# Four units' query scores in one group, a 16-bit pair look-up, both attentions' queries by token

## The chip, the cores and the metric

The program runs on one core of one Trainium2 chip. A core has a matrix engine (PE, TensorE; its weight loads are PEld), a vector engine (DVE), a scalar engine (ACT), GpSimd (POOL) and SyncE (SP), which here only issues DMAs. Each engine takes its instructions strictly in the order of its own queue and waits on semaphores. The metric is the device time of one execution in microseconds; lower is better.

## The reference

Two transformer layers follow each other on 256 tokens of width 1024, in fp32. The change touches the first.

```python
h = concat([meta_tokens(16), x(256), zeros])                      # 272 tokens count
proj = rms_norm(h, attn_norm) @ w_in                              # c_q, c_kv, k_rope, dq, dk, dv
y_mla  = softmax(rope(norm(q)) @ rope(norm(k)).T * s) @ v         # 8 heads of 96, q from c_q (256 wide)
y_diff = (softmax(q1 k1 + bias) - lam * softmax(q2 k2 + bias)) @ v   # 4 heads, 2 x 64 each, q = norm(dq)
h = h + concat([y_mla, y_diff]) @ w_out
# PEER, on xn = rms_norm(h):
q = (xn @ w_query).reshape(.., 8, 2, 128)                         # 8 heads, two sides
s = einsum(q, sub_keys)                                           # 128 keys a side
s1, i1 = top_k(s[side 0], 16);  s2, i2 = top_k(s[side 1], 16)
best, flat = top_k(s1[:, None] + s2[None, :], 16)                 # of 256 sums
e1 = take(i1, flat // 16);  e2 = take(i2, flat % 16)              # the look-up
act = gelu(xn . u[e1 * 128 + e2]);  h = h + (softmax(best) * act) . v[...]
```

The queries of all heads (q of the MLA, dq of the differential attention) are wanted for 256 tokens, the keys for 272. `take` picks, for each of 128 slots of a token and each side, one of 16 indices.

## The kernel before

The weights stream through in 399 units of 512 KB. `unit` (called for each) issues the DMA into `raw` (4 buffers), ACT or DVE rounds it to fp32r as `wh`, and DVE or POOL makes the rest `wl = raw - wh` (3 buffers each). A product of fp32 accuracy is three fp32r products (`mm3`: hi*hi, hi*lo, lo*hi). A unit of the kind `_stat` is stationary and yields features on partitions (moving operand: 256 or 272 tokens); one of the kind `_mov` is the moving operand (512 columns) and yields tokens on partitions.

Stages in order of time: the input products and both attentions (0 to 165 us); `wq`, the PEER queries in 16 units (169 to 227 us); 90 of the 128 `u` units, with the routing (top 16 and look-up) and then the gates beside them on DVE; the other `u` and all `v` units; then the second layer.

`Flow` records every operation (so all of them have line 683) and `schedule` writes each engine's queue before the run: it walks a model time, takes for each engine the ready operation of the lowest priority (place in the program, some biases), with costs from `_cost`. `ORDER` is the program order of the attention's generators (`dq`, `q`, `m`, `V` are the diff queries, MLA queries, MLA heads, dv units). `Side` lays pieces of a generator between the `u` units: each `yield` gives a rough cost, and `side.step(2.1)` grants so much per unit.

What the change touches:

- `pair_norm("dq")`: 4 stationary units; for each the square on ACT, two fp32 products with 2 columns for the sums by head, then spreading of the norms by transposes (PE) and 4 multiplications (DVE).
- `queries`: per MLA head 6 products with `uq` stationary, a DVE multiplication with the rope table, a square on ACT, two one-column fp32 products for the sums.
- `values` and `mla_head`: the values of the first 16 keys stand on partitions 0 to 15 of `mv[:, 0]`. For each head the weights of these keys are transposed (2 transposes into the g bank), copied by DVE, and multiplied with `mv[:, 0]` (2 fp32 products of 64 columns), beside 3 transposes and 3 products for the other keys; then a reciprocal and a scaling.
- `wq`: after each unit ACT copies the result to `t`, and 2 fp32 products with the sub-keys write the scores (`s<-s,t`); ACT takes the scores out after every fourth unit.
- `routing`: look-up per half of the tokens and side: `is_equal` (128x2048 fp32), a product with the indices (128x2048 fp32), a sum over 16.
- `tok_norm` (3 calls with `rows`): `squares` leaves two halves, and `total` adds them in PE with 4 one-column products.

Of the kernel before, what the change touches and what calls it, by code (L numbers as in the profile page):

```python
# [125 lines left out]
def _units(i):  # L126
# [3 lines left out]
    kr = w[:, 512:544]  # L130
    kr = np.concatenate([kr, kr[:, _SWAP]] * 2, 1)
    r = uq[:, :, 64:]
    r = np.concatenate([r, r[:, :, _SWAP]], 2)
    even, odd = np.concatenate([uq[:, :, :64], r], 2), np.concatenate([r, uq[:, :, :64]], 2)
    uq = np.concatenate([(odd if h % 2 else even)[:, h] for h in range(8)], 1)
# [8 lines left out]
    return {  # L144
        "dk": _stat(w[:, 1056:1568]), "dq": _stat(w[:, 544:1056]), "dv": np.concatenate([_mov(w[:, 1568:1824]), _mov(w[:, 1824:2080])], 0),
        "ckv": _stat(w[:, 256:512]), "kr": _stat(kr), "cq": _stat(w[:, 0:256]),
        "ukn": _stat(c(ukv[:, :, :64]).reshape(256, 512)), "uv": _mov(c(ukv[:, :, 64:]).reshape(256, 512)),
        "uq": _stat(uq), "woa": _stat(wo[:512]), "wob": _stat(wo[512:]),
        "xk": _stat(kv[:, :256]), "xv": _mov(kv[:, 256:]),
# [18 lines left out]
def _vec_list(i):  # L168
# [9 lines left out]
    two = lambda v: np.concatenate([v, v])[:, None]  # L178
    rope = lambda v: np.concatenate([v[64:], v[64:][_SWAP]] * 2)[:, None]
    rb = np.zeros((P, 4), np.float32)  # L180
# [44 lines left out]
def _consts():  # L225
# [19 lines left out]
    cos, sin = np.cos(ang).T, np.sin(ang).T  # L245
    e["cs"] = np.concatenate([cos, cos, -sin, sin] * 2, 0).astype(f)
    d = S - 1 - np.arange(NR)
# [131 lines left out]
class Flow:  # L379
# [129 lines left out]
    def schedule(self):  # L509
# [53 lines left out]
        while done < len(ops):  # L563
            progress = False
            for e in self.real:
# [128 lines left out]
def _build(tc, nc, ctx, A, O):  # L694
# [378 lines left out]
    def values():  # L1073
        wh, wl = mov(unit("uv"), 512)
        for c in range(3):
            o = bank("d")
            for k in range(2):
                mm3(o, ckh[:, k, VC[c]], ckl[:, k, VC[c]], wh[:, k], wl[:, k], k == 0, k == 1)
            if c == 0:
                G.memset(mv[:, 0], 0.0)  # L1080
            n = P if c else NM
            SC.activation(mv[:n, c], o[:n], AF.Copy)
            yield


    mr = sm(32)

    def queries():
        acc = bank("g")
        for h in range(8):  # L1090
            if h % 4 == 0:
                wh, wl = unit("uq")
            o = bank("d")[:, :T]
            for k in range(2):
                mm3(o, wh[:, 2 * (h % 4) + k], wl[:, 2 * (h % 4) + k], cqh[:, k], cql[:, k], k == 0, k == 1)
            V.tensor_mul(mq[:, h], o, tq[h % 2])
            q = square(o, T)
            for c, sl in enumerate(TT):
                PE.matmul(acc[:, 8 * c + h:8 * c + h + 1], q[:, sl], c_("indb" if h % 2 else "inda"),
                          start=h == 0 and c == 0, stop=h == 7 and c == 1, skip_group_check=True)  # L1100
            yield
        inv_sqrt(mr[:, 0:16], acc[:, :16], 1.0, E96)
        V.tensor_scalar(mr[:, 16:32], mr[:, 0:16], -1.0, None, op0=OP.mult)
        yield

    lam = sm(8)
# [37 lines left out]
    def mla_head(hd):  # L1144
        w = tmp[:, 1056 * (hd % 4):1056 * (hd % 4) + 1056]
        s, st = bank("s"), fl.tile([P, 16], F32, "hs")
        es = []
        for q in range(2):
            n = NB[q]
            sq = s[:, 144 * q:144 * q + n]  # L1150
            PE.matmul(sq, mq[:, hd, TT[q]], mk[:, hd, :n], start=True, stop=True)
            e = w[:, 144 * q:144 * q + n]
            soft(e, sq, mask[:, S - n:S], mr[:, 16 + 8 * q + hd:17 + 8 * q + hd], st[:, q:q + 1], st[:, 2 + q:3 + q])
            es.append(e)
        V.reciprocal(st[:, 4:6], st[:, 2:4])
        b = bank("g")
        weigh(b, 256, 64, es[0], es[1], mv, slice(64 * hd, 64 * hd + 64), w)
        z = st[:, 4:6].rearrange("p (c f) -> p c f", (P, 2, 1), f=1).to_broadcast([P, 2, 64])
        V.tensor_tensor(om[:, :, 64 * hd:64 * hd + 64], by_head(b[:, 256:384], 2, 64), z, op=OP.mult)

# [71 lines left out]
    def mla_heads():  # L1232
        for hd in range(8):
            mla_head(hd)
            if hd % 2:
                mla_out(hd // 2)
            yield
# [17 lines left out]
    def half_dense(*args):  # L1255
        for _ in half_units(*args):
# [3 lines left out]
    parts = {"dk": pair_norm("dk", dk, gd[:, 0:1], ALL, S, VC, KT, em, "s"),  # L1260
             "dq": pair_norm("dq", dq, 0.125, XS, T, TT, QT, em[:, 1:3], "p"), "k": keys(), "v": values(), "q": queries(),
             "K": rotated(), "C": latents(), "b": distances(), "L": lambdas(), "m": mla_heads(), "V": dv_units(),
# [39 lines left out]
    ab_i = small[:, 1536:2048].bitcast(U32)  # L1302
    i1f, abf = small[:, 2048:2560], small[:, 2560:3072]
    e12, wgt = small[:, 3072:3584], small[:, 3584:3840]
    one_i32 = c_("iota")

    def slots(j, n=1):
# [9 lines left out]

    ps_s = None
# [25 lines left out]
    def routing():  # L1344
        for c in range(2):
            for g in range(16):
                o = 256 * c + 16 * g
                top16(s_[c][:, g], s1[:, o:o + 16], i1[:, o:o + 16])
                yield 1.0
            V.tensor_copy(i1f[:, 256 * c:256 * c + 256], i1[:, 256 * c:256 * c + 256])  # L1350
            sv = s1[:, 256 * c:256 * c + 256].rearrange("p (h s k) -> p h s k", (P, 8, 2, 16), h=8, s=2)
# [12 lines left out]
            V.tensor_copy(abf[:, 256 * c:256 * c + 256], ab_i[:, 256 * c:256 * c + 256])  # L1364
            iv = i1f[:, 256 * c:256 * c + 256].rearrange("p (h s k) -> p h s k", (P, 8, 2, 16), h=8, s=2)
            for side in range(2):
                x = abf[:, 256 * c + 128 * side:256 * c + 128 * side + 128]
                hot = cand[c].flat.rearrange("p (s j) -> p s j", (P, 128, 16), s=128)
                V.tensor_tensor(hot, one_i32[:, 0:16].rearrange("p (o j) -> p o j", (P, 1, 16), o=1).to_broadcast([P, 128, 16]),
                                x.rearrange("p (s o) -> p s o", (P, 128, 1), o=1).to_broadcast([P, 128, 16]), op=OP.is_equal)  # L1370
                yield 2.3
                cv = cand[c].flat.rearrange("p (h a b) -> p h a b", (P, 8, 16, 16), h=8, a=16)
                V.tensor_tensor(cv, cv, iv[:, :, side, :].rearrange("p h (o k) -> p h o k", (P, 8, 1, 16), o=1)
                                .to_broadcast([P, 8, 16, 16]), op=OP.mult)
                yield 2.3
                V.reduce_sum(out=e12[:, 256 * c + 128 * side:256 * c + 128 * side + 128], in_=hot, axis=AX.X)
                yield 2.3
# [546 lines left out]
```

## Time and profile before

| what | value |
|---|---|
| median of 3 runs | 1346.52 us (1344.83 to 1346.79) |
| the profiled execution: its own time, its span | 1346.25 us, 1344.1 us |
| PE, DVE, ACT, POOL busy | 1324.5, 978.6, 722.1, 65.9 us |
| chain that ended last | PE 87%, DVE 7%, the rest 1% each or less |
| mean granted clock of PE | 0.997 of full speed |

PE's busy time is the union of its instructions, each shown from its start to its modelled end. Since they are pipelined, neighbours overlap: the distance between starts is what an instruction costs PE, and the recorded 0.28 us of a product is more than that. A product of two fp32 operands (not fp32r) appears as two records; a transpose as one. Where a wait is under some tenths of a microsecond, it is seen only as a larger distance between starts, not as idle time.

### The profile page before, as it was taken

To read this page: it belongs to the slowest core of one execution; us is meant where nothing else is said; L and a number is where in the kernel's file an instruction comes from. 1 tells how busy PE (TensorE), PEld (TensorE's weight loads), DVE (VectorE), ACT (ScalarE), POOL (GpSimd) and SP (SyncE) were. 2 spreads that over 40 slices of the span, in tenths; PEclk is the share of its full clock that TensorE was granted. 3 is DMA by queue.
4 is the path that set the end of the run, shared out by engine and by line. 5 is a ranking of instruction groups with operands and counts; after the bars stand their busy time and mean duration, and the time that the engine had idled before them with its cause. 6 is when DMAs were issued, how large, how long until landed. Compare 5 with 4: busy or idle time off the path is not lost.

```text
span 1344.1 us, 23753 instructions
## 1 busy us (share of the span) xinstructions
PE 1324.5 (99%) x9270; PEld 1205.1 (90%) x9270; DVE 978.6 (73%) x1833; ACT 722.1 (54%) x1222; POOL 65.9 (5%) x31
## 2 busy tenths in 40 slices
PE   9999999999999999999999999999999999999997
PEld 8898899999999999889999888888889798999996
DVE  7555789998498877985655555575576678978886
ACT  6445545435466665454544444444555546755555
POOL 0000001445200000000000000000000000000000
PEclk9999999999999999999999999999999999999999
DMA  6342344555587779995655555575545244465553
GB/s 236 120 143 79 108 145 143 171 184 180 171 282 258 259 267 347 364 309 188 202 188 189 187 188 187 187 249 187 186 163 185 82 152 153 144 198 185 177 184 98
DMA packets 101048, 256.29 MB, mean 191 GB/s; under 512 B 7940, under 2 KB 42696, under 8 KB 100808
## 3 DMA queue, kind: packets, MB, share of 16 engines
q1 hardware_dynamic: 95216, 236.62, 54.2%
q10 hardware_dynamic: 5720, 18.17, 3.4%
q8 instruction: 72, 1.18, 0.4%
q14 instruction: 40, 0.33, 0.1%
HBM read 236.86 MB, written 17.83 MB: 189 GB/s over the span
## 4 chain that ended last, share of the span: by engine, by line
PE 87%; DVE 7%; DMA 1%; ACT 1%; issue 1%; ACTq 0%; DVEq 0%
PE d L683 30%; PE acc L683 26%; PE g L683 5%; PE ua L683 4%; PE ug L683 4%; PE facc L683 4%; DVE s L683 4%; PE s L683 3%; PE wq L683 3%; DVE wl L683 2%; PE p L683 2%; DMA raw<-st 1%; PE dq L683 1%; PE mq L683 1%; PE mk L683 1%
## 5 line engine op out<-in xcount | busy, mean ns | idle before, releaser
L683 DVE TENSOR_TENSOR wl<-raw,wh 128x1024 fp32r<-128x1024 f32 x385 | 474.0, 1233 | 188.8 <-ACT wh L683 187.3
L683 ACT ACTIVATE wh<-raw 128x1024 fp32r<-128x1024 f32 x399 | 420.9, 1056 | 350.6 <-PE d L683 193.2
L683 PE MATMUL d<-ah,wl 128*128 128x256 f32 x1088 | 308.7, 284 | 3.9 <-DVE wl L683 3.6
L683 PE MATMUL d<-ah,wh 128*128 128x256 f32 x1088 | 309.9, 285 | 0.4 <-DVE h L683 0.3
L683 PE MATMUL d<-al,wh 128*128 128x256 f32 x1088 | 307.8, 283 | 0.8 <-DVE al L683 0.8
L683 PEld LDWEIGHTS d<-ah,wl 128*128 128x128 f32 x1088 | 205.9, 189 | 6.3 <-DVE wl L683 5.1
L683 PEld LDWEIGHTS d<-ah,wh 128*128 128x128 f32 x1088 | 206.0, 190 | 2.3 <-DVE h L683 0.7
L683 PEld LDWEIGHTS d<-al,wh 128*128 128x128 f32 x1088 | 205.9, 189 | 2.1 <-DVE al L683 1.0
L683 PE MATMUL acc<-wh,ch 128*128 128x512 f32 x512 | 203.4, 397 | 0.0
L683 PE MATMUL acc<-wl,ch 128*128 128x512 f32 x512 | 203.4, 397 | 0.0
L683 PE MATMUL acc<-wh,cl 128*128 128x512 f32 x512 | 202.2, 395 | 0.0
L683 ACT ACTIVATE ch<-s 128x256 fp32r<-128x256 f32 x149 | 62.0, 417 | 170.0 <-PE acc L683 166.6
L683 DVE TENSOR_TENSOR cl<-s,ch 128x256 fp32r<-128x256 f32 x149 | 63.2, 425 | 76.0 <-ACT ch L683 75.8
L683 PEld LDWEIGHTS acc<-wh,cl 128*128 128x128 f32 x512 | 96.5, 188 | 23.4
L683 PEld LDWEIGHTS acc<-wh,ch 128*128 128x128 f32 x512 | 96.5, 189 | 22.8
L683 PEld LDWEIGHTS acc<-wl,ch 128*128 128x128 f32 x512 | 96.4, 188 | 21.5
L683 POOL TENSOR_TENSOR wl<-raw,wh 128x1024 fp32r<-128x1024 f32 x22 | 61.9, 2814 | 287.5 <-PE wq L683 222.1
L683 DVE TENSOR_TENSOR s<-s,s 128x256 f32<-128x256 f32 (+5 forms) x142 | 55.8, 446 | 0.5 <-ACT s L683 0.3
L683 DVE TENSOR_TENSOR s<-s 128x2048 f16<-128x2048 f16 (+4 forms) x47 | 53.3, 1136 | 0.8
L683 POOL TENSOR_TENSOR s<-s 128x512 f32<-128x512 f32 x2 | 2.5, 1284 | 983.3 <-ACT s L683 983.3
L683 ACT ACTIVATE s<-d 128x512 f32<-128x512 f32 (+1 forms) x71 | 41.4, 583 | 15.4 <-PE d L683 15.3
L683 PE MATMUL ua<-al,wh 128*128 128x256 f32 x168 | 47.6, 283 | 0.2 <-DVE al L683 0.2
(307 smaller groups left out, 2374.4 us busy)
## 6 DMA issues: line engine op xcount, KB each, us to landing
raw<-st SPq DMA_DIRECT2D x407, 512.0 KB, 3.6
gd<-u ACTq DMA_DIRECT2D x32, 512.0 KB, 5.2
s<-gd SPq DMA_DIRECT2D x16, 1024.0 KB, 8.8
h<-xt SPq DMA_DIRECT2D x2, 512.0 KB, 6.5
s<-sk SPq DMA_DIRECT2D x1, 1024.0 KB, 5.0
u<-mt SPq DMA_DIRECT2D x4, 256.0 KB, 4.9
o<-s SPq DMA_DIRECT2D x3, 256.0 KB, 2.9
s<-ear SPq DMA_DIRECT2D x1, 664.0 KB, 6.2
```

Of the source, the lines that this page charges most:

```text
L683: f(*[real(a) for a in o.args], **{k: real(a) for k, a in o.kw.items()})
```

## The change

1. `wq`: the scores of four units are computed after the fourth, 8 products in a row.
2. Look-up: indices and one-hot rows are fp16, two slots interleaved (`iot` holds each number twice), so that `is_equal` and the product work on 128x2048 fp16; the sum reads the pairs with a stride and writes fp32 as before. The side grants are 1.75 per unit in the routing and 2.4 in the gates (both 2.1 before).
3. `queries` and `diff_queries`: `uq` and `dq` are moving operands. The MLA queries come out by token (two units of 512 columns), DVE copies them, ACT squares, DVE sums by head, then 16 transposes bring each head back to features, and DVE multiplies with the rope table from PSUM. The diff queries accumulate in two p banks over four units, are normed by two DVE multiplications, transposed (8) and copied out by ACT.
4. `values`: the first 32 key columns stand four times side by side, so the values of the first keys land on the partitions 32i to 32i+15. `mla_head` lays down four heads' results in one g bank; after the fourth, the four heads' first-key weights are gathered (2 DVE copies), transposed (2), copied, and multiplied in 2 products of 256 columns; one reciprocal and one scaling serve four heads.
5. `tok_norm` with `rows`: DVE adds the two halves of the squares, PE has 2 one-column products instead of 4.
6. `ORDER` follows the new yields; the planner adds 130 ns to single-input DVE operations while POOL works.

```diff
-ORDER = "... dk dk k v b k v q k v q dk dk dq q q dq q q dq q dk dk dq q q dq dq m dq m m dq m V m m V ..."
+ORDER = "... dk dk k v b k v q k v q dk dk dq q dq q dq dk dk dq q q dq m dq m m dq m V m m V ..."
+                elif e == "v" and o.meth in SINGLE and shared["g"] > now:
+                    cost += 130.0
@@ tok_norm
         sq = squares(x, T, KD, 2, r[:, 2:3])
+        if rows:
+            V.tensor_add(sq[0], sq[0], sq[1])
+            sq = sq[:1]
@@ queries
-            o = bank("d")[:, :T]
-            for k in range(2):
-                mm3(o, wh[:, 2 * (h % 4) + k], wl[:, 2 * (h % 4) + k], cqh[:, k], cql[:, k], k == 0, k == 1)
+            for c in range(2):
+                o = bank("d")
+                for k in range(2):
+                    mm3(o, cqh[:, k, TT[c]], cql[:, k, TT[c]], wh[:, k], wl[:, k], k == 0, k == 1)
+                V.tensor_copy((om, oo)[u][:, c], o)
+                at = 8 * c + 4 * u
+                by_head_sums(o, acc[:, at:at + 4].rearrange("p (a b) -> p a b", (P, 2, 2), a=2), 4, 128, paired)
...
+            for c in range(2):
+                PE.transpose(o[:, TT[c]], (om, oo)[h // 4][:, c, P * (h % 4):P * (h % 4) + P], ident)
             V.tensor_mul(mq[:, h], o, tq[h % 2])
-            q = square(o, T)
-            for c, sl in enumerate(TT):
-                PE.matmul(acc[:, 8 * c + h:8 * c + h + 1], q[:, sl], c_("indb" if h % 2 else "inda"),
@@ mla_head, after the fourth head (i == 3)
+            for c in range(2):
+                PE.transpose(pm[:, TT[c]], ml[:, TT[c]], ident)
+            V.tensor_copy(pms, pm)
+            for c in range(2):
+                PE.matmul(b[:, T * c:T * c + T], pms[:, TT[c]], mv[:, 0, at:at + T], start=False, stop=c == 1, ...)
@@ wq
-        if g % 4 == 0:
-            ps_s = [bank("s") for _ in range(2)]
-        for c in range(2):
-            PE.matmul(ps_s[c][:, (g % 4) * P:(g % 4 + 1) * P], qt[:, TT[c]], skt[:, g], start=True, stop=True)
-        if g % 4 == 3:
+        qts.append(qt)
+        if g % 4 == 3:
+            ps_s = [bank("s") for _ in range(2)]
+            for c in range(2):
+                for i in range(4):
+                    PE.matmul(ps_s[c][:, i * P:i * P + P], qts[g - 3 + i][:, TT[c]], skt[:, g - 3 + i], start=True, stop=True)
@@ routing, look-up
-                V.tensor_tensor(hot, one_i32[:, 0:16]...to_broadcast([P, 128, 16]), x...to_broadcast([P, 128, 16]), op=OP.is_equal)
+                V.tensor_tensor(hot, iot[:, 0:16]...to_broadcast([P, 64, 16, 2]), x, op=OP.is_equal)
-        side.step(2.1)
+        side.step(2.4 if side.gates else 1.75)
```

Where the instructions move. First PE in the middle of `wq`: `wq` rows are products of a unit, `s<-...,t` the scores. Before:

```order
L683 MATMUL wq<-ah,wh 128x256
L683 MATMUL wq<-al,wh 128x256
L683 MATMUL s<-s_1440,t 128x128 x2
L683 MATMUL wq<-ah,wl 128x256
L683 MATMUL wq<-ah,wh 128x256
```

and now:

```order
L685 MATMUL wq<-al,wh 128x256
L685 MATMUL wq<-ah,wl 128x256
L685 MATMUL s<-s_1293,t 128x128 x8
L685 MATMUL wq<-ah,wh 128x256
L685 MATMUL wq<-al,wh 128x256
```

The scores of a unit stood two products into the next one, 16 times; the scores of four units now stand right behind the last product of the fourth, four times.

Second DVE at the first look-up, early in the `u` units (`s_1440` and `s_1293` hold the sums and then the one-hot rows, `s_1975` and `s_1846` the indices and results; a `wl` is the split of a weight unit that PE waits for). Before:

```order
L683 TENSOR_TENSOR wl<-raw,wh 128x1024
L683 TENSOR_TENSOR s_1440<-s_1440,s_1975 128x2048
L683 TENSOR_REDUCE s_1975<-s_1440 128x128
L683 TENSOR_TENSOR wl<-raw,wh 128x1024
L683 TENSOR_TENSOR s_1440<-cst,s_1975 128x2048
L683 TENSOR_TENSOR wl<-raw,wh 128x1024
L683 TENSOR_TENSOR s_1440<-s_1440,s_1975 128x2048
L683 TENSOR_REDUCE s_1975<-s_1440 128x128
L683 TENSOR_TENSOR wl<-raw,wh 128x1024
```

and now:

```order
L685 TENSOR_TENSOR wl<-raw,wh 128x1024
L685 TENSOR_TENSOR s_1293<-s_1293,s_1846 128x2048
L685 TENSOR_REDUCE s_1846<-s_1293 128x128
L685 TENSOR_TENSOR wl<-raw,wh 128x1024
L685 TENSOR_TENSOR s_1293<-iot,s_1846 128x2048
L685 TENSOR_TENSOR s_1293<-s_1293,s_1846 128x2048
L685 TENSOR_REDUCE s_1846<-s_1293 128x128
L685 TENSOR_TENSOR wl<-raw,wh 128x1024
```

The second side's three operations now stand between two splits, where a split stood between the first and the second of them; counted from the start of `wq` the first multiplication comes one DVE split later.

Third PE among the MLA heads (`p<-cst` and `g<-cst` are transposes, `g<-s_71,s_123` the products with the values, `d<-w..` the dv units). Before:

```order
L683 MATMUL g<-s_71,s_123 128x64 x5
L683 MATMUL p<-cst,s_123 128x128 x2
L683 MATMUL g<-cst,s_123 128x128
L683 MATMUL p<-cst,s_123 128x128 x3
L683 MATMUL d<-wh,s_104 128x256 x2
L683 MATMUL p<-cst,s_123 128x128 x2
L683 MATMUL g<-s_71,s_123 128x64 x5
```

and now, at the end of the first four heads:

```order
L685 MATMUL g<-s_71,s_123 128x256 x2
L685 MATMUL d<-wl,s_104 128x256
L685 MATMUL p<-cst,s_123 128x128
L685 MATMUL d<-wh,s_104 128x256
L685 MATMUL s<-s_71 128x272
L685 MATMUL p<-cst,s_123 128x128 x2
L685 MATMUL g<-cst,s_71 128x128 x4
```

Each head had five products of 64 columns; now it has three, and two of 256 columns serve four heads. The four transposes `g<-cst,s_71` of the heads' outputs stand one scaling (DVE) behind them.

## Rows read from the trace of the kernel before

**Rows 1.** The page: busy time, share of the span and records of each engine.
```profile
PE 1324.5 (99%) x9270; PEld 1205.1 (90%) x9270; DVE 978.6 (73%) x1833; ACT 722.1 (54%) x1222; POOL 65.9 (5%) x31
```

**Rows 2.** Stretches: length, busy PE, PEld, DVE, ACT, POOL (records), clock, DMA, GB/s.
```profile
87.00:125.00 38.00, 37.99 (x309) 36.37 (x309) 22.02 (x79) 20.19 (x57) 0.00 (x0) 1.00 0.34 109
155.00:160.00 5.00, 4.86 (x26) 4.65 (x26) 2.30 (x6) 1.17 (x3) 0.00 (x0) 0.66 0.36 105
169.00:226.00 57.00, 57.00 (x452) 53.93 (x452) 51.39 (x220) 28.14 (x48) 1.95 (x1) 1.00 0.46 149
226.00:277.00 51.00, 47.60 (x397) 46.99 (x396) 50.93 (x158) 25.59 (x32) 20.65 (x9) 1.00 0.49 155
360.00:510.00 150.00, 150.00 (x1513) 149.31 (x1512) 125.21 (x110) 90.77 (x191) 0.00 (x0) 1.00 0.75 258
775.00:800.00 25.00, 25.00 (x108) 20.12 (x107) 14.59 (x19) 12.32 (x18) 0.00 (x0) 1.00 0.57 188
```

**Rows 3.** PE by form: out<-in, shape xcount | busy us, mean ns | idle before.
```profile
L683 PE MATMUL s<-s,t 128*128 128x128 f32 x64 | 11.4, 301 | 0.4 <-ACT t L683 0.4
...
L683 PE MATMUL g<-s,s 128*128 128x64 f32 x80 | 9.7, 270 | 0.0
...
L683 PE MATMUL g<-cst,t 128*128 128x1 f32 x36 | 4.9, 240 | 0.0
```

**Rows 4.** PE among the MLA heads: start, us, engine, what xcount.
```profile
93.53 0.62 PE L683 MATMUL s<-s 128*128 128x272 f32 x2
93.99 0.27 PE L683 MATMUL p<-cst,s 128*128 128x128 f32 x1
94.10 1.23 PE L683 MATMUL g<-s,s 128*128 128x64 f32 x10
```

**Rows 5.** PE in `wq`, one unit's period.
```profile
192.26 0.71 PE L683 MATMUL s<-s,t 128*128 128x128 f32 x4
...
192.93 0.28 PE L683 MATMUL wq<-ah,wh 128*128 128x256 f32 x1
...
195.54 0.28 PE L683 MATMUL wq<-al,wh 128*128 128x256 f32 x1
195.82 0.38 PE L683 MATMUL s<-s,t 128*128 128x128 f32 x1
```

**Rows 6.** The chain of waits at the look-up: start, us, what.
```profile
214.86 2.02 DVE s L683 x9
...
267.33 1.90 DVE wl L683
...
273.68 3.02 DVE wl L683
```

**Rows 7.** PE in the `u` units at the look-up; idle before, and its releaser.
```profile
269.29 0.39 PE L683 MATMUL d<-ah,wl 128*128 128x256 f32 x1 [1.50 <-DVE wl L683]
...
276.74 0.39 PE L683 MATMUL d<-ah,wl 128*128 128x256 f32 x1 [1.49 <-DVE wl L683]
```

**Rows 8.** DVE by form: the look-up, the gates, the splits.
```profile
L683 DVE TENSOR_TENSOR wl<-raw,wh 128x1024 fp32r<-128x1024 f32 x385 | 474.0, 1233 | 188.8 <-ACT wh L683 187.3
...
L683 DVE TENSOR_TENSOR s<-iot,s 128x2048 f16<-128x2048 f16 x32 | 37.8, 1218 | 0.0
...
L683 DVE TENSOR_TENSOR s<-cst,s 128x2048 f32<-128x2048 f32 x4 | 11.1, 2785 | 0.0
...
L683 DVE TENSOR_REDUCE s<-s 128x128 f32<-128x2048 f32 x4 | 9.1, 2286 | 0.1
L683 DVE TENSOR_TENSOR s<-s 128x2048 f32<-128x2048 f32 x4 | 9.1, 2280 | 0.0
```

**Rows 9.** POOL's split and DVE's first `is_equal`, side by side.
```profile
260.07 2.56 POOL L683 TENSOR_TENSOR wl<-raw,wh 128x1024 fp32r<-128x1024 f32 x1 [3.30 <-ACT wh L683]
...
260.49 4.28 DVE L683 TENSOR_TENSOR s<-cst,s 128x2048 f32<-128x2048 f32 x1
```

**Rows 10.** PE before the clock fell, behind the diff heads.
```profile
153.25 0.41 PE L683 MATMUL g<-cst,s 128*128 128x128 f32 x2 [0.72 <-DVE s L683]
...
154.99 0.39 PE L683 MATMUL d<-al,wh 128*128 128x256 f32 x1 [0.79 <-DVE al L683]
```

More of the change, by code (lines that the diff above doesn't have):

```diff
@@ L1074, in values @@
         wh, wl = mov(unit("uv"), 512)
+        first = [fl.tile([P, T], F32R, tag) for tag in ("ch", "cl")]
+        for d, a in zip(first, (ckh, ckl)):
+            SC.activation(d.rearrange("p (k o c) -> p k o c", (P, 2, 4, 32), k=2, o=4),
+                          a[:, :, 0:32].rearrange("p k (o c) -> p k o c", (P, 2, 1, 32), o=1).to_broadcast([P, 2, 4, 32]), AF.Copy)
         for c in range(3):
@@ L1077, in values @@
             for k in range(2):
-                mm3(o, ckh[:, k, VC[c]], ckl[:, k, VC[c]], wh[:, k], wl[:, k], k == 0, k == 1)
-            if c == 0:
+                if c:
+                    xh, xl = ckh[:, k, VC[c]], ckl[:, k, VC[c]]
+                else:
+                    xh, xl = (a[:, P * k:P * k + P] for a in first)
+                mm3(o, xh, xl, wh[:, k], wl[:, k], k == 0, k == 1)
+            if c:
+                SC.activation(mv[:, c], o, AF.Copy)
+            else:
                 G.memset(mv[:, 0], 0.0)
-            n = P if c else NM
@@ new lines, in paired @@
+    def paired(q):
+        return q.via(lambda a: bass.AP(tensor=a.tensor, offset=a.offset, ap=[a.ap[0], [256, 2], [160, 2], [1, 96]]), (P, 2, 2, 96))
+    def queries():
+        acc = fl.tile([P, 32], F32, "acc")
+        for u in range(2):
+            wh, wl = mov(unit("uq"), 512)
+            for c in range(2):
[5 more added lines that the diff above has]
+                by_head_sums(o, acc[:, at:at + 4].rearrange("p (a b) -> p a b", (P, 2, 2), a=2), 4, 128, paired)
+            if u:
+                inv_sqrt(mr[:, 0:16], acc[:, :16], 1.0, E96)
+                V.tensor_scalar(mr[:, 16:32], mr[:, 0:16], -1.0, None, op0=OP.mult)
+            yield
+        for h in range(8):
+            if h % 2 == 0:
+                b = bank("g")
+            o = b[:, T * (h % 2):T * (h % 2) + T]
+            for c in range(2):
+                PE.transpose(o[:, TT[c]], (om, oo)[h // 4][:, c, P * (h % 4):P * (h % 4) + P], ident)
+            V.tensor_mul(mq[:, h], o, tq[h % 2])
+            if h % 2:
+                yield
@@ new lines, in diff_queries @@
+    def diff_queries():
+        acc, qt = fl.tile([P, 32], F32, "acc"), Grid(tmp[:, 2944:2944 + 1024], (2, 512))
+        o = [bank("p") for _ in range(2)]
+        for u in range(4):
+            wh, wl = mov(unit("dq"), 512)
+            for c in range(2):
+                for k in range(2):
+                    kk = 2 * u + k
+                    mm3(o[c], nh[:, kk, NM + P * c:NM + P * c + P], nl[:, kk, NM + P * c:NM + P * c + P], wh[:, k], wl[:, k], kk == 0, kk == 7)
+                if u == 3:
+                    by_head_sums(o[c], acc[:, 8 * c:8 * c + 8], 8, 64, lambda q: by_head(q, 8, 64))
@@ L1101, in queries @@
             yield
-        inv_sqrt(mr[:, 0:16], acc[:, :16], 1.0, E96)
-        V.tensor_scalar(mr[:, 16:32], mr[:, 0:16], -1.0, None, op0=OP.mult)
+        r = inv_rms(acc, 2, 8, 1.0 / 64, em[:, 1:3])
+        for c in range(2):
+            V.tensor_tensor(by_head(qt[:, c], 8, 64), by_head(o[c], 8, 64),
+                            r[:, 8 * c:8 * c + 8].rearrange("p (c f) -> p c f", (P, 8, 1), f=1).to_broadcast([P, 8, 64]), op=OP.mult)
         yield
+        for j in range(0, 4, 2):
+            b = bank("p")
+            for i in range(2):
+                for c in range(2):
+                    PE.transpose(b[:, T * i + P * c:T * i + P * c + P], qt[:, c, P * (j + i):P * (j + i) + P], ident)
+            SC.activation(dq[:, j:j + 2], b.rearrange("p (a b) -> p a b", (P, 2, T), a=2), AF.Copy, scale=0.125)
+            yield
@@ L1152, in mla_head @@
             e = w[:, 144 * q:144 * q + n]
[L1153 to L1159, printed above, removed]
+            soft(e, sq, mask[:, S - n:S], mr[:, 16 + 8 * q + hd:17 + 8 * q + hd], st[:, 4 * q + i:4 * q + i + 1],
+                 st[:, 8 + 4 * q + i:9 + 4 * q + i])
+            for m in range(q + 1):
+                PE.transpose(pt[:, (q + m) * P:(q + m + 1) * P], e[:, NM + m * P:NM + m * P + P], ident)
+        SC.activation(pts, pt[:, :3 * P], AF.Copy)
+        for c in range(2):
+            o = b[:, T * c + 64 * i:T * c + 64 * i + 64]
+            for m in range(c + 1):
+                PE.matmul(o, pts[:, (c + m) * P:(c + m + 1) * P], mv[:, 1 + m, 64 * hd:64 * hd + 64],
+                          start=m == 0 and i == 0 and c == 0, stop=False, skip_group_check=True)
+        if i == 3:
+            pm, pms, ml = bank("s")[:, :T], w[:, 800:1056], tmp[:, 800:1056]
+            for c in range(2):
+                a = tmp[:, 0:4224].rearrange("p (h f) -> p h f", (P, 4, 1056), h=4)[:, :, 144 * c:144 * c + 32]
+                V.tensor_copy(ml[:, TT[c]].rearrange("p (h f) -> p h f", (P, 4, 32), h=4), a)
+            for c in range(2):
+                PE.transpose(pm[:, TT[c]], ml[:, TT[c]], ident)
+            V.tensor_copy(pms, pm)
+            at = 64 * hd - 192
+            for c in range(2):
+                PE.matmul(b[:, T * c:T * c + T], pms[:, TT[c]], mv[:, 0, at:at + T], start=False, stop=c == 1, skip_group_check=True)
+            V.reciprocal(st[:, 8:16], st[:, 8:16])
+            z = st[:, 8:16].rearrange("p (c h f) -> p c h f", (P, 2, 4, 1), c=2, h=4).to_broadcast([P, 2, 4, 64])
+            V.tensor_tensor(om[:, :, at:at + T].rearrange("p c (h f) -> p c h f", (P, 2, 4, 64), h=4),
+                            b.rearrange("p (c h f) -> p c h f", (P, 2, 4, 64), c=2, h=4), z, op=OP.mult)
     def mla_out(j):
@@ L1234, in mla_heads @@
             mla_head(hd)
-            if hd % 2:
-                mla_out(hd // 2)
+            if hd % 4 == 3:
+                for j in range(hd // 2 - 1, hd // 2 + 1):
+                    mla_out(j)
             yield
@@ L1260, in _build @@
     parts = {"dk": pair_norm("dk", dk, gd[:, 0:1], ALL, S, VC, KT, em, "s"),
-             "dq": pair_norm("dq", dq, 0.125, XS, T, TT, QT, em[:, 1:3], "p"), "k": keys(), "v": values(), "q": queries(),
+             "dq": diff_queries(), "k": keys(), "v": values(), "q": queries(),
              "K": rotated(), "C": latents(), "b": distances(), "L": lambdas(), "m": mla_heads(), "V": dv_units(),
@@ L1322, in _build @@
         SC.activation(qt, o, AF.Copy)
[L1323 removed]
+        qts.append(qt)
+        if g % 4 == 3:
             ps_s = [bank("s") for _ in range(2)]
[L1325 to L1327 removed]
+            for c in range(2):
+                for i in range(4):
+                    PE.matmul(ps_s[c][:, i * P:i * P + P], qts[g - 3 + i][:, TT[c]], skt[:, g - 3 + i], start=True, stop=True)
             for c in range(2):
```

75 lines of the change are left out of this document (43 added, 32 removed).

## Prediction

> **What bounds the kernel now.** I read the page first: PE is busy in 99% of the span, DVE in 73%, ACT in 54% [rows 1]. So an instruction taken from PE's queue is worth its time, unless PE then waits for something. Then the stretches, to see where that second clause holds [rows 2]. Among the MLA heads (87 to 125 us) PE is busy throughout and DVE 22 of 38 us: PE is the limit, with latencies under it. In `wq` (169 to 226 us) PE is busy throughout and DVE already 51.4 of 57 us. In the first third of the `u` units (226 to 277 us) it turns over: DVE is busy 50.9 of 51 us and PE misses 3.4. The chain of waits agrees: from 214.86 us it runs on DVE until a split of 3.02 us ends at 276.7 [rows 6]. The page's share of 73% says nothing of that; it is a mean over stages with different limits.
>
> Last I looked for what an instruction costs PE. The distance between starts is the price: 22 products of 256 columns lie between 192.93 and 195.54 us, so 0.119 us each [rows 5]; 108 of 512 columns fill 25 us, 0.231 each [rows 2]; ten fp32 records of 64 columns last 1.23 us with the last one's 0.27, so 0.11 each; a transpose 0.11 (93.99 to 94.10) and an fp32 record of 272 columns 0.23 (93.53 to 93.99, two records) [rows 3, 4]. An fp32 product is two records, so even one with a single column costs 0.22 us.
>
> **Attention, terms on PE.** Out go the products for the sums by head: 8 of the diff queries and 16 of the MLA queries, 48 records by 0.11 = 5.3 us; 16 products for the first keys, 32 records, 3.5 us; 16 transposes for them, 1.8 us. In come 4 products of 256 columns, 8 records by 0.23 (the row of 272 is the nearest) = 1.8 us; 4 transposes for the first keys and 16 for the MLA queries, 2.2 us. The 8 transposes of the diff queries replace 8 that spread the norms. The two query products keep their columns: 144 by 0.119 = 17.1 us become 72 by 0.231 = 16.6. Net: -10.6 + 4.0 - 0.5 = -7.1 us.
>
> DVE gets four copies, six sums over 512 columns, and loses copies and small scalings; ACT about breaks even. In the head stretch DVE has 16 us to spare, so I cost that at nothing by itself. What it may cost is latency: the MLA queries now pass PE, DVE, PE before their rope product; the diff queries pass ACT, DVE, ACT, DVE before their transposes, and hold both p banks until then, for which the heads' transposes wait, and PE's queue behind those; and twice a group of four heads ends in transposes, a copy, two products, one scaling, four transposes. In the order dv products stand in all these places, a few of them between the scaling and its transposes, so only the rest of a latency shows. For a wait of this kind behind a DVE chain the trace has 0.72 and 0.79 us [rows 10]. Four places by 0.75 are 3.0 us. The bounds are no wait (-7.1) and waits that eat it all (0); I take -7.1 + 3.0 = -4.1, since 0.75 is from the poorest-covered place of the same stage.
>
> **wq.** A unit's period is 195.82 - 192.26 = 3.56 us [rows 5]. 24 products by 0.119 are 2.85, four score records 0.44; 0.27 is left. Of it 0.16 lies ahead of the score (195.54 to 195.82, less 0.12): it stands two products behind the unit's end and waits for ACT's copy, too briefly to be listed at full size (the form has 0.4 us of idle time in all [rows 3]). In the new order the scores of the three earlier units, six records or 0.66 us, stand ahead of the fourth's, which covers the same copy. 16 by 0.27 = 4.3 us go, 4 by 0.11 for the return to fp32r stay: -3.9. If the new place exposes the copy again, 4 by 0.5 come back (-1.9).
>
> **Look-up.** PE's two idle pieces are 1.50 and 1.49 us, both ended by a split on DVE [rows 7]: 3.0 us is all that can be had here on PE, whatever DVE saves. DVE must also take up `wq`'s 3.9 us, since its work there stays while PE arrives earlier: 6.9 us to be taken off DVE's queue up to the split that ended the second wait. What leaves that queue: the first `is_equal` shrinks from 4.28 us [rows 9] to the 1.22 us that the same form costs in the gates; the multiplication (2.28) and the sum (2.29) come one split later [rows 8]. That is 3.1 + 4.6 = 7.6 us, just over 6.9, so the wait goes with little to spare. I take -2.5 of the 3.0. What is late next is again DVE, a few tenths behind, then PE. Later DVE has room in both kernels, and the further halved operations hide behind PE.
>
> A price in this is a clash. POOL's split starts at 260.07 and lasts 2.56 us; the `is_equal` that starts at 260.49 ends at 264.77, which is POOL's end plus 2.14, about the 2.28 of an unhindered operation of that size [rows 8, 9]. The next two splits on DVE last 1.90 and 3.02 us on the chain where 1.23 is the mean [rows 6, 8]. [...]
>
> **The rest.** `tok_norm`: 6 products less, 12 records, 1.3 us; each call has a DVE addition more on its way, hidden behind products except perhaps ahead of the second layer's FFN; -0.9 (bounds -1.3 and 0). The gates get 2.4 instead of 2.1: by the order their pieces stand ahead of units 68 to 98 instead of 64 to 98. DVE is busy 125.2 of 150 us there [rows 2]; times 35/31 that is 94%, so PE still hides it: 0. If it were over 100%, each per cent would be 1.3 us.
>
> **Sum.** -4.1 - 3.9 - 2.5 - 0.9 = -11.4 on the profiled execution's 1346.25 us (span 1344.1 and 2.1 around it), 0.3 under the median: 1334.8, so 1335 us. Its own range is 1332 to 1338.
>
> **Rivals.**
> A, attention gives nothing: the cover was the removed work itself, and the new chains wait as long. For it: those chains are longer than any that the queries had. Against: the dv products between. 1346.25 - 3.9 - 2.5 - 0.9 = 1339.
> B, DVE stays the limit from `wq` to the look-up: the three clashes come again (4.28, 1.90 and 3.02 instead of about 2.2, 1.2 and 1.2: 4.6 us), or the pair form runs no faster than fp32. Then the 7.6 falls to 3 or less, and `wq`'s 3.9 and the 3.0 turn into waiting for splits: 1346.25 - 4.1 - 0.9 = 1341. For it: no spare on DVE. Against: the gates' form at 1.22 us, and fewer routing pieces per unit (1.75 against 2.1).
> C, slower: the clashes spread. Nine units from the 17th to the 33rd are split on POOL; if each blocked a DVE operation by 2.1 us as at 260 us, DVE would be 19 us late, 0.7 are spare, and PE would get 18 us of waiting: 1353. It decides against the change from about 1.6 us per split (14.8 in all). Against it: the splits before 260 us did not block anything that the chain shows.
> [...]
> E, everything hides: -7.1 - 4.3 - 3.0 - 1.3 = -15.7, 1330.5.
>
> **How the numbers follow.** Likeliest 0.50, A 0.17, B 0.13, C 0.04, D 0.06, E 0.10. 1330 to 1342 takes in all but C and the ends of B, D and E: 8 in 10. About 2.7 us (0.2%) is what a measurement of this kernel can tell from no change. Faster by more (under 1343.8): all of the likeliest, A and E, most of B and D, 0.90. Within: the end of B and D, 0.05. Slower: C and what I have not thought of, 0.05.
>
> **What would show it.** In the changed profile: starts of `wq` products at 0.119 us through four units, and 64 score records in four blocks without 0.16 us ahead; no idle PE piece over 0.5 us ended by a split between `wq` and the 36th unit; `is_equal` and its multiplication at about 1.2 us, the strided sum at 2.3; the first `wq` product some 4 us earlier than 169.1; a clock of 1.00 up to 150 us. Wrong if the first `wq` product is not earlier (A), if PE waits for splits in the `u` units (B, C), or if the gates end PE's full stretch.

## The result and the profile after

The changed kernel takes 1330.52 us (median of 5 runs, 1330.02 to 1332.78) against 1346.02: a ratio of 0.9884, 95% interval [0.987, 0.9899]. The forecast was 1335, with 1330 to 1342. The time lies at the lower edge of that range, and below the forecast's own 1332 to 1338. The profiled execution took 1330.02 us, its span is 1328.2 us.

The page and the stretches, in the columns of [rows 1, 2]; the stages now begin earlier:

```profile
PE 1306.7 (98%) x9118; PEld 1191.8 (90%) x9118; DVE 968.0 (73%) x1823; ACT 725.4 (55%) x1219; POOL 66.1 (5%) x33
```

```profile
160.00:213.00 53.00, 53.00 (x445) 52.40 (x444) 50.30 (x209) 28.50 (x48) 1.30 (x1) 1.00 0.47 152
226.00:277.00 51.00, 51.00 (x432) 51.00 (x432) 48.26 (x132) 23.41 (x27) 24.79 (x9) 1.00 0.57 181
360.00:510.00 150.00, 148.72 (x1484) 147.13 (x1483) 126.48 (x121) 92.19 (x193) 0.00 (x0) 1.00 0.81 268
745.00:945.00 200.00, 200.00 (x876) 164.12 (x875) 124.92 (x162) 99.56 (x147) 0.00 (x0) 1.00 0.63 202
```

PE no longer idles between 226 and 277 us, where it missed 3.4 us before. It idles a little in the gates (360 to 510 us), where it did not. And in the long stretch of 512-column products it starts more of them in the same time. The kernel before, in that stretch:

```profile
745.00:945.00 200.00, 200.00 (x856) 161.02 (x855) 122.11 (x159) 97.70 (x144) 0.00 (x0) 1.00 0.61 197
```

The counts are 856 and 876 products in 200 us, and the mean distance between two starts is 0.234 and 0.229 us, at a clock of 1.00 in both. No line of the diff is about these products.

Stages between the starts of the first product of each kind in the two traces:

| stage | before, us | after, us | difference |
|---|---|---|---|
| start to the first `wq` product | 168.94 | 160.84 | -8.1 |
| `wq` to the last scores | 58.59 | 54.40 | -4.2 |
| `u` units to the first `acc` product | 292.18 | 290.93 | -1.2 |
| `acc` products (`v`, rest of `u`) | 472.03 | 468.41 | -3.6 |
| second layer to the first `ua` product | 155.69 | 155.30 | -0.4 |
| first `ua` to first `ug` product | 5.28 | 6.78 | +1.5 |
| the rest | 191.44 | 191.58 | +0.1 |

They add up to the 15.9 us between the spans. The timeline of PE shows the waits in the attention of the changed kernel: the last two are those of [rows 10], the first is the only new one of that size. The fourth row is the first `wq` product.

```profile
139.68 0.39 PE L685 MATMUL d<-ah,wh 128*128 128x256 f32 x1 [0.60 <-DVE h L685]
...
145.16 0.41 PE L685 MATMUL g<-cst,s 128*128 128x128 f32 x2 [0.72 <-DVE s L685]
...
146.90 0.39 PE L685 MATMUL d<-al,wh 128*128 128x256 f32 x1 [0.79 <-DVE al L685]
...
160.84 0.28 PE L685 MATMUL wq<-ah,wh 128*128 128x256 f32 x1
```

In `wq` the eight score products of four units (16 records) follow the last product by 0.12 us, so the wait of 0.16 us of [rows 5] is gone; the return costs 175.04 - 172.99 - 0.12 - 16 times 0.11 = 0.17 us:

```profile
172.99 0.28 PE L685 MATMUL wq<-ah,wl 128*128 128x256 f32 x1
173.11 2.17 PE L685 MATMUL s<-s,t 128*128 128x128 f32 x16
175.04 0.36 PE L685 MATMUL wq<-ah,wh 128*128 128x256 f32 x1
```

DVE by form, as in [rows 8]. Four operations of each of the first two forms are the look-up, four of the third its sums:

```profile
L685 DVE TENSOR_TENSOR s<-iot,s 128x2048 f16<-128x2048 f16 x36 | 42.6, 1220 | 0.0
L685 DVE TENSOR_TENSOR s<-s 128x2048 f16<-128x2048 f16 x34 | 41.6, 1224 | 0.7
...
L685 DVE TENSOR_REDUCE s<-s 128x128 f32<-128x2048 f16 x4 | 9.1, 2286 | 0.1
```

The pair form takes 1.22 us and the strided sum 2.29, as forecast. By the prediction that is what ended the waits of [rows 7]; the experiments say otherwise.

### The profile page after: what moved, and what is told of

Its sections match the earlier page's. It is cut to its first block, busy times and chain, and to the rows that moved or that the text cites. A ratio compares the mean times of both kernels' runs of the same rounds, so it can differ in the third digit from the quotient of the medians.

```text
span 1328.2 us, 23420 instructions
## 1 busy us (share of the span) xinstructions
PE 1306.7 (98%) x9118; PEld 1191.8 (90%) x9118; DVE 968.0 (73%) x1823; ACT 725.4 (55%) x1219; POOL 66.1 (5%) x33
## 4 chain that ended last, share of the span: by engine, by line
PE 86%; DVE 6%; DMA 2%; ACT 1%; issue 1%; SPq 0%; ACTq 0%; DVEq 0%
PE d L685 33%; PE acc L685 25%; PE ug L685 4%; PE facc L685 4%; PE ua L685 4%; PE g L685 4%; DVE s L685 4%; PE p L685 2%; PE s L685 2%; DMA raw<-st 2%; DVE wl L685 2%; PE wq L685 1%; PE mq L685 1%; PE mk L685 1%; ACT wh L685 1%
## 5 line engine op out<-in xcount | busy, mean ns | idle before, releaser
L685 DVE TENSOR_TENSOR wl<-raw,wh 128x1024 fp32r<-128x1024 f32 x383 | 468.5, 1225 | 205.2 <-ACT wh L685 203.5
L685 PE MATMUL ua<-ah,wl 128*128 128x256 f32 x168 | 47.7, 284 | 1.4 <-DVE wl L685 1.4
```

The lines of the kernel that those rows point to most:

```text
L685: f(*[real(a) for a in o.args], **{k: real(a) for k, a in o.kw.items()})
```

## The experiments

Three questions were open: why 512-column products got cheaper, whether the savings of attention and `wq` are independent, and what took the two waits at the look-up away. Each run shares its "before" with the others of its group (medians 1346.53, 1346.31 and 1346.50).

The clock adds scatter between executions. In most of the profiled ones the granted clock is 0.50 instead of 1.00 in one to three stretches of some 3.4 us before the end of the FFN, each worth 1.7 us by estimate (half of 3.4), and they change place from run to run: one at 155.8 us in the kernel before, one at 147.6 in the changed kernel, none in e3, three in e5. So a difference of 1 to 2 us between medians is read together with the stage where it should stand.

**e1, the changed kernel with `cl` at its old place; e2, the kernel before with `cl` at the new one.** The compiled program lays the buffers of the SBUF pool in the order of their first use. In the changed kernel `values` is the first to use `cl`, and so `cl` stands at byte 198656 of a partition instead of 224384.

```diff
-        first = [fl.tile([P, T], F32R, tag) for tag in ("ch", "cl")]      # e1
+        first = [fl.tile([P, T], F32R, tag) for tag in ("ch", "ch")]
```

```diff
         wh, wl = mov(unit("uv"), 512)                                     # e2, kernel before
+        first = [fl.tile([P, T], F32R, tag) for tag in ("ch", "cl")]
+        for d, a in zip(first, (ckh, ckl)):
+            SC.activation(d.rearrange(...), a[:, :, 0:32]...to_broadcast([P, 2, 4, 32]), AF.Copy)
```

> The changed kernel, but the copy of the first keys' low part takes its tile from the pool `ch` instead of `cl`. No instruction is added or removed; only the three `cl` buffers are laid where the kernel before had them (byte 224384 of a partition instead of 198656). Theory P (place): a product of 512 columns costs what the place of its stationary `cl` in SBUF makes it cost. Then the 1536 products of 512 columns go back from 0.229 to 0.234 us in the stretch 745 to 945 us, +7 us, the products of 256 columns win back up to 2 us, and the time is 1335 to 1338 against 1330.5. Rival O (order): the price follows from the order of products and banks, or is noise between executions; then 0.229 stays and the time is within 1 us of 1330.5.

> The kernel before, with two small ACT copies of the first 32 key columns into a `ch` and a `cl` tile that nothing reads: they only make `cl` the earlier allocation, so that its buffers lie where the changed kernel has them. Theory P (place): 512-column products fall from 0.234 to about 0.229 us, -7 us, 256-column ones lose up to 2: 1339 to 1342 against 1346.0, without any part of the change. Rival O: no difference, 1346 plus at most 1 for the two copies.

e1: 1335.28 us (0.9914 [0.9896, 0.9931]), 4.8 over the changed kernel. e2: 1341.69, 4.8 under before (ratio 0.9957 [0.9942, 0.9972]), without a part of the change. First e1's stretch, then e2's (750 to 950 us):

```profile
745.00:945.00 200.00, 200.00 (x857) 160.95 (x855) 122.28 (x159) 97.28 (x142) 0.00 (x0) 1.00 0.62 199
```

```profile
750.00:950.00 200.00, 200.00 (x875) 164.11 (x875) 124.74 (x163) 99.99 (x146) 0.00 (x0) 1.00 0.61 202
```

857 and 875 products: the price moves with the place, in both directions, and theory P holds. In e2 the `acc` stage is 5.8 us shorter than before, the rest of the FFN 0.7 longer. In e1 the stage is 3.8 us longer than in the changed kernel, though 1.5 us of that kernel's waits for splits are missing there.

An early `cl` also moves what lies behind it: in every run with the lower price `h1`, `ah`, `al` and three small buffers lie 3072 bytes higher. In the stretch from 745 to 945 us no instruction of any engine reads or writes one of them; of the buffers that are used there (`raw`, `wh`, `wl`, `ch`, `cl` and areas of the gates) only `cl` has moved in e1 and e2.

**e3, part 1 alone** (the scores of four units; the diff is that of `wq` above).

> The kernel before with part 1 alone (the scores of four units in one group of eight products). Theory D (the prediction's account of the look-up): DVE is the limit from `wq` to the look-up, so the 4 to 5 us that `wq` saves on PE come back as longer waits for splits: `wq` ends 4 to 5 us earlier, the two waits at 269 and 277 us together grow from 3.0 to 7 us or more, and the time stays within 1 us of 1346.0. Rival T (the savings are independent): the waits stay about 3 us and the time is 1341 to 1342.

1342.98 us (0.9978 [0.9967, 0.9989]), -3.5. `wq` takes 54.96 instead of 58.59 us, and the two waits keep their size, 3.7 us earlier:

```profile
265.56 0.39 PE L683 MATMUL d<-ah,wl 128*128 128x256 f32 x1 [1.49 <-DVE wl L683]
...
273.01 0.39 PE L683 MATMUL d<-ah,wl 128*128 128x256 f32 x1 [1.49 <-DVE wl L683]
```

Theory D falls: DVE moves along when the scores come earlier, so `wq`'s saving doesn't turn into waiting. The prediction had DVE take up 3.9 us that it never had to.

**e4, part 2 alone** (look-up and grants).

> The kernel before with part 2 alone (16-bit look-up, grants of 1.75 and 2.4). Theory D: both waits of 1.5 us go, nothing else moves, 1343 (-3.0), and DVE has about 4 us to spare at that place. Rival B of the prediction: the pair form is no faster or is blocked as long by the splits on POOL; at least one wait stays, 1344.5 to 1346. If the gates' grants cost something, a new wait shows after 355 us and takes 1 to 1.5 us of it back (the changed kernel has one of 1.4 us at 366 us).

1352.57 us (1.0041 [1.0025, 1.0056]): 6.0 slower. None of the theories expected that. The wait that the expectation allowed for in the gates came:

```profile
385.86 0.39 PE L683 MATMUL d<-ah,wh 128*128 128x256 f32 x1 [1.28 <-ACT s L683]
```

And there are five waits for splits instead of two:

```profile
268.06 0.39 PE L683 MATMUL d<-ah,wl 128*128 128x256 f32 x1 [1.48 <-DVE wl L683]
...
281.31 0.39 PE L683 MATMUL d<-ah,wl 128*128 128x256 f32 x1 [1.46 <-DVE wl L683]
...
288.77 0.39 PE L683 MATMUL d<-ah,wl 128*128 128x256 f32 x1 [1.50 <-DVE wl L683]
...
301.90 0.39 PE L683 MATMUL d<-ah,wl 128*128 128x256 f32 x1 [1.48 <-DVE wl L683]
...
315.30 0.39 PE L683 MATMUL d<-ah,wl 128*128 128x256 f32 x1 [1.75 <-DVE wl L683]
```

Behind the fourth stand these two, POOL's split and DVE's:

```profile
298.39 2.38 POOL L683 TENSOR_TENSOR wl<-raw,wh 128x1024 fp32r<-128x1024 f32 x1 [2.22 <-ACT wh L683]
```

```profile
298.56 3.28 DVE L683 TENSOR_TENSOR wl<-raw,wh 128x1024 fp32r<-128x1024 f32 x1
```

DVE comes 0.17 us after POOL and ends 1.07 us after it, so its 1.23 us of work lasts 3.28. Behind the first three waits, too, stands a split that DVE began after one of POOL's (1.81 to 2.82 us long); the fifth has its usual length, but comes late behind three operations of the look-up. The first `is_equal` began 0.95 us behind POOL's split of 258.85 us, and for all its 16 bits it takes 3.18 us instead of 1.22:

```profile
259.80 3.18 DVE L683 TENSOR_TENSOR s<-iot,s 128x2048 f16<-128x2048 f16 x1
```

In the changed kernel DVE is ahead of POOL. First POOL's, then DVE's rows:

```profile
260.04 2.40 POOL L685 TENSOR_TENSOR wl<-raw,wh 128x1024 fp32r<-128x1024 f32 x1 [3.29 <-ACT wh L685]
```

```profile
257.19 1.23 DVE L685 TENSOR_TENSOR wl<-raw,wh 128x1024 fp32r<-128x1024 f32 x1 [0.65 <-ACT wh L685]
258.33 1.22 DVE L685 TENSOR_TENSOR s<-s,s 128x2048 f16<-128x2048 f16 x1
259.59 2.29 DVE L685 TENSOR_REDUCE s<-s 128x128 f32<-128x2048 f16 x1
262.89 1.23 DVE L685 TENSOR_TENSOR wl<-raw,wh 128x1024 fp32r<-128x1024 f32 x1 [1.02 <-ACT wh L685]
```

Here only the sum, with one input, runs beside POOL, and both keep their usual length (2.29 and 2.40 us). The next split of POOL shows the other order: DVE's multiplication in 16 bits (265.29 us) begins 0.45 us ahead of it and keeps 1.23 us, and POOL's split lasts 3.03 instead of 2.40. Again POOL's row first:

```profile
265.74 3.03 POOL L685 TENSOR_TENSOR wl<-raw,wh 128x1024 fp32r<-128x1024 f32 x1 [3.31 <-ACT wh L685]
```

```profile
265.29 1.23 DVE L685 TENSOR_TENSOR s<-s,s 128x2048 f16<-128x2048 f16 x1
```

So in these rows the place of DVE's operation with two inputs sets how long it lasts: ahead of POOL's split 1.23 us, behind it 3.28 (the split) and 3.18 (`is_equal`, in 16 bits too). This is rival C's mechanism, which the prediction thought 0.04 likely. Part 2 brings the 16 bits and the grants of 1.75 and 2.4 together; which of them made the further waits was not tried on the kernel before.

**e5, the changed kernel without the planner's 130 ns; e6, the kernel before with them.**

```diff
                 elif o.both:                                  # e5 removes these two lines,
                     shared["v"] = now + cost                  # e6 adds them
+                elif e == "v" and o.meth in SINGLE and shared["g"] > now:
+                    cost += 130.0
```

> The changed kernel without the planner's 130 ns (part 6): only the order of the queues moves. Theory N: it is this term, not the 16 bits, that takes routing off DVE's queue ahead of the splits (in the order some 4 to 8 us less of it stand ahead of the splits of the 28th to 42nd unit with the term than without). Then waits for splits of 1.6 us come up between 250 and 310 us as in the kernel with the look-up alone (five there), DVE's splits beside POOL's last 1.8 to 3.3 us, and the time is 1336 to 1340 against 1330.5. Theory L (the prediction's account): the 16-bit look-up has freed DVE; then the time stays within 1 us of 1330.5.

> The kernel before with the planner's 130 ns alone: no instruction differs, only the order. Theory N: both waits of 1.5 us at 269 and 277 us go, no split on DVE between 226 and 280 us lasts over 1.5 us, 1343 to 1344. Theory L: they stay, within 1 us of 1346.5.

e6: 1343.71 us (0.9985 [0.9974, 0.9997]), -2.6 without an instruction changed. No idle piece of PE is left between 226 and 277 us:

```profile
226.00:277.00 51.00, 51.00 (x430) 51.00 (x431) 47.53 (x153) 25.52 (x30) 24.55 (x9) 1.00 0.54 172
```

One sign that theory N named did not come: two splits on DVE last over 1.5 us there. The first takes 1.53 us at 268.53; the second began behind one of POOL's and takes 2.69. First POOL's row, then DVE's:

```profile
270.33 4.45 POOL L685 TENSOR_TENSOR wl<-raw,wh 128x1024 fp32r<-128x1024 f32 x1 [1.34 <-ACT wh L685]
```

```profile
273.18 2.69 DVE L685 TENSOR_TENSOR wl<-raw,wh 128x1024 fp32r<-128x1024 f32 x1 [0.65 <-ACT wh L685]
```

PE doesn't wait for it all the same. So the new order doesn't end the clash; here the split was early enough that PE had not come to it.

e5: 1334.42 us (0.991 [0.9895, 0.9925]), 3.9 over the changed kernel, less than was expected: one wait comes back, of 2.3 us, not several.

```profile
259.12 0.39 PE L683 MATMUL d<-ah,wl 128*128 128x256 f32 x1 [2.31 <-DVE wl L683]
```

Behind it the granted clock fell; the stretch has a mean of 0.97, by estimate one piece of 3.4 us at 0.50, which cost 1.7:

```profile
226.00:277.00 51.00, 48.69 (x398) 48.49 (x397) 50.63 (x139) 21.12 (x25) 25.18 (x9) 0.97 0.54 170
```

Theory L falls in both runs. Theory N's cause holds: the order, not the 16 bits, took the waits away. Its size in e5 does not (1336 to 1340 us and several waits were expected). Where POOL splits, the planner now thinks DVE's routing steps longer and lays fewer of them ahead of each split. By the 29th split (DVE's and POOL's, counted from 6 us ahead of the first `wq` product) DVE has done 85.7 us of other work in the kernel before, 85.7 in e4, 77.8 in e6 and 80.0 in the changed kernel (sums of DVE's rows).

**e7, parts 3 and 4 alone** (queries by token, first keys of four heads).

> The kernel before with parts 3 and 4 (queries by token, first keys of four heads), which also brings `cl` to the place that was worth 4.8 us by itself. The prediction: first `wq` product 4.1 us earlier (164.8 us in the profile), so 1346.5 - 4.1 - 4.8 = 1337.6. Rival W (no new waits, as the changed kernel's trace reads): 7 to 8 us earlier (161 to 162 us), 1334 to 1335. Rival A: not earlier, 1341.7.

1332.98 us (0.991 [0.9897, 0.9922]), -13.3, of which 4.8 belong to `cl`'s place (e2): -8.5. The first `wq` product:

```profile
160.84 0.28 PE L683 MATMUL wq<-ah,wh 128*128 128x256 f32 x1
```

8.1 us earlier than the 168.94 of the kernel before. Rival W holds, A is out, the forecast's 3.0 us of waiting did not come.

**e8, the changed kernel with the fp32 look-up; e10, with the 16-bit look-up, but grants of 2.1.** e8 takes part 2 of the diff back, e10 only its last line:

```diff
-        side.step(2.4 if side.gates else 1.75)
+        side.step(2.1)
```

> The changed kernel with the look-up in fp32 and the grants of 2.1 as before; the 130 ns stay. Theory N: with the routing in the order that the 130 ns make, the longer look-up hides too; at most one wait for a split of 1.5 us, and the wait at 366 us (1.4 us, if the gates' grant of 2.4 makes it) goes: 1329 to 1332. Theory L: DVE is the limit again, two or more waits of 1.5 us and more, 1334 to 1338.

> The changed kernel with 2.1 per unit in the routing and in the gates; the look-up stays in 16 bits. Theory G: the waits at 366 us (1.4 us) and at 513, 551 and 575 us (0.9, 0.5, 0.9 us) come from the gates' grant of 2.4; they go, and the time is 1328 to 1329, as with the look-up in fp32 at 2.1. Rival: they come from the 16-bit look-up's place in the order; then they stay, 1330.5 or more.

e8: 1329.02 us (0.9878 [0.9862, 0.9893]); e10: 1328.34 (0.9869 [0.9853, 0.9886]). The look-up's 16 bits are worth nothing that these runs can tell, and the grants of 1.75 and 2.4 cost some 2 us by the medians, whose intervals overlap. The stages show it more clearly: from the first `wq` to the last `acc` product the two kernels with these grants (the changed one and e9 below) take 811.6 and 811.4 us, e8 and e10 take 807.4 and 807.8. Of these 4 us e10 loses 1.0 again in the second layer, by two new waits of 0.62 and 0.45 us ahead of `ua`. Three of the waits that the changed kernel has and neither of these shows are

```profile
366.52 0.39 PE L685 MATMUL d<-ah,wh 128*128 128x256 f32 x1 [1.28 <-ACT s L685]
...
512.88 0.39 PE L685 MATMUL d<-ah,wl 128*128 128x256 f32 x1 [0.76 <-DVE wl L685]
...
575.13 0.39 PE L685 MATMUL d<-ah,wl 128*128 128x256 f32 x1 [0.76 <-DVE wl L685]
```

Theories N and G hold. e10 sets both grants back, so that the part of each is not told apart. In e8 the longer operations are hidden, with DVE full and PE not idle:

```profile
226.00:277.00 51.00, 51.00 (x432) 51.00 (x431) 50.05 (x121) 23.26 (x28) 26.51 (x9) 1.00 0.57 178
```

**e9, the long norm sums ahead of the FFN alone.**

```diff
-        if rows:
+        if rows and short:          # short=False in the last call
             V.tensor_add(sq[0], sq[0], sq[1])
```

> The changed kernel with the long norm sums (part 5) only in the last of the three calls, ahead of the second layer's FFN. Theory F: there the order puts a product in front of its split, which costs 1.5 us; first `ua` to first `ug` product goes from 6.78 back to 5.28 us, 1329.0 against 1330.5. Rival: DVE's addition itself was the price; then that stretch falls by 0.4 at most.

1329.28 us (0.9871 [0.9853, 0.9889]); `ua` to `ug` is 5.28 us again. The median moved by 1.2 us, with runs from 1326.41 to 1330.34, so the stage is the evidence rather than the median. In the changed kernel, PE:

```profile
1133.77 0.54 PE L685 MATMUL g<-cst,u 128*128 128x1 f32 x4
...
1136.30 0.38 PE L685 MATMUL ua<-ah,wl 128*128 128x256 f32 x1 [1.42 <-DVE wl L685]
1136.52 0.38 PE L685 MATMUL g<-cst,sm 128*128 128x128 f32 x2
1136.66 0.36 PE L685 MATMUL ug<-ah,wh 128*128 128x256 f32 x1
```

and in e9:

```profile
1133.05 1.02 PE L685 MATMUL g<-cst,u 128*128 128x1 f32 x8
1135.05 0.40 PE L685 MATMUL g<-cst,sm 128*128 128x128 f32 x2
1135.21 0.36 PE L685 MATMUL ug<-ah,wh 128*128 128x256 f32 x1
```

The shorter sums save 0.48 us of PE there. But DVE's addition moves the splits back, and the order has the second `ua` unit's first product with `wl` ahead of the spread (`g<-cst,sm`) and of 24 `ug` products; it waits 1.42 us for its split. Theory F holds.

**e11, the fp32 look-up and the long sums ahead of the FFN together; e12, e11 with `cl` beside `raw`.**

```diff
     G.memset(zero.bitcast(F32), 0.0)
+    G.memset(fl.tile([P, T], F32R, "cl").bitcast(F32), 0.0)      # e12
```

> The changed kernel without part 2 (look-up in fp32, grants of 2.1) and with the long norm sums ahead of the FFN. If both edits add up, 1329.0 - 1.5 = 1327.5, under both kernels; if the FFN's wait comes from what stands before it, 1329.

> The kernel of the run before, with a GpSimd memset of one `cl` tile at the start, so that the `cl` buffers lie at byte 86720, below `raw`, and `raw` to `t` 3072 bytes higher. Theory P: the price of a 512-column product takes a third value, somewhere between its least interval of 0.226 and 0.234 us (1536 times 3 ns less would be 5 us: 1322.5; 5 ns more 7 us: 1335). Rival: only the place at the end (224384) is dear; then 0.229 stays and the time is that of the run before.

e11: 1325.60 us (0.9846 [0.9833, 0.986]), under both kernels. By the medians that is 4.9 under the changed kernel, more than the 1.5 and 1.2 of e8 and e9 alone; by the stages the two edits add up, 3.4 us from `wq` to the last `acc` product and 1.5 from `ua` to `ug`. e12: 1323.97 (0.9835 [0.9821, 0.9848]), but not by a third price:

```profile
745.00:945.00 200.00, 200.00 (x876) 164.21 (x875) 124.60 (x163) 100.22 (x146) 0.00 (x0) 1.00 0.62 201
```

876 products, as in the changed kernel. Its runs (1322.81 to 1325.05) overlap e11's (1324.30 to 1326.15); that the 1.6 us are the place's was not shown.

## Why the prediction came out as it did

The sign, the bottleneck and the price list (but for the products of 512 columns) were right, and the range held the time; the sum of 11.4 us was 4 to 5 short. That the time lies in the range is in part luck: the misses below go both ways. Without the one term that the prediction did not see, the kernel takes 1335.28 us (e1), the forecast of 1335 almost to the point, and yet three of the sum's four terms were wrong in size or cause, and the gates, put at 0, were not 0. By its own steps:

- **Attention, -4.1: mis-sized.** The waits, "four places by 0.75", were sized from the place with the poorest cover [rows 10]. The trace has one new wait of 0.60 us, at none of the four places, and the stage became 8.1 us shorter (e7). The bound "no wait", -7.1, was the nearer end. What the stage gained beyond that bound, 1 us and the 0.6 of the new wait, is spread over small differences and was not traced.
- **`wq`, -3.9: right.** -4.2 in the changed kernel, -3.5 alone (e3). The new place does cover the copy.
- **Look-up, -2.5: right in size at the waits, wrong in cause.** Both waits went, but the step "what leaves that queue" credited the 16-bit operations (3.1 + 4.6 us). Without the rest of the change, they and their grants make the kernel 6 us slower (e4), where the first `is_equal` takes 3.18 us and not 1.22, and without them nothing is lost (e8). The planner's 130 ns, which the prediction did not price at all, moved the order of DVE's queue; alone it removes both waits (e6), and without it one comes back (e5). It should have been read from DVE's order with that line and without it. That DVE "must also take up `wq`'s 3.9 us" was wrong too (e3).
- **`tok_norm`, -0.9: the exception that the text named, "perhaps ahead of the second layer's FFN", was not priced.** There the edit costs 1.5 us, a loss outside the bounds of -1.3 and 0. The call ahead of it gains 0.4 (second layer up to `ua`), so the two calls of the second layer lose 1.1 together; the first was not measured apart.
- **Gates, 0: wrong by some 2 us** (e10; both grants together, 3.8 in the stages that they touch). DVE's mean share left room, as argued, but the first wait is for an ACT copy (366.52), and the others come later, from 512 us on. The prediction's own sign, "if the gates end PE's full stretch", came.
- **Not seen: the price of a 512-column product.** The sum took 0.231 us, counted over 25 us, as fixed. Over 200 us it is 0.234 before, and it fell to 0.229 by the place of `cl`, worth 4.8 us (e1, e2), the second largest term.

Rival E's 1330.5 is nearly the time measured, yet not for its reason: not everything hid. 4.8 us from the place of a buffer made up for 1.5 at the FFN and 2 or more from the grants. Rival B is out, since PE waits for no split at the look-up; a loss to the clock in the attention (D) is out as well, as the granted clock falls to 0.50 there once in the changed kernel (3.4 us from 147.6) and once in the kernel before (3.4 us from 155.8), behind the same two waits. Of C the mechanism is real (3.18 and 3.28 us in e4, 2.69 in e6), and in the changed kernel the order keeps it from PE.

## What to carry to other kernels

When a change goes along with edits to a planner's costs, price the order that comes out apart from the operations: build the order with the one and without the other, and count what stands ahead of the instruction that waits. An edit that saves PE time in front of a strict queue can still cost, if one product moves ahead of its operand (here 0.48 us saved and 1.42 waited). And a new first use of a pool moves buffers: a steady price that nobody touched may then move too (here from 0.234 to 0.229 us), so look at the count of products in an undisturbed stretch first.

## What was not expected of the hardware

In these runs the price of a 512-column fp32r product goes with where in SBUF one of its stationary operands lies: 856 or 857 products in 200 us with `cl` at byte 224384, 875 or 876 with it at 198656 or 86720, at the same full clock and with PE busy throughout. In the kernel before the distances between starts repeat over nine products, from 0.225 to 0.240 us (mean 0.234), in the changed one over six, from 0.225 to 0.232 (mean 0.229), and in e12 over three with the same mean; so it is a steady pattern, not a wait now and then. What makes it was not tried and stays open: `cl`'s own address, or how it lies to the other operands.
